# A two-layer hybrid transformer in fp32 on one core: low parts and sums of the FFN moved from GpSimd to VectorE, and the gate product put behind an addition

## The chip, the cores and the metric

The kernel runs on one core of a Trainium2 chip. The number that counts is the device time of one execution in microseconds. A core has five engines with an instruction queue each: TensorE (PE in the rows; its weight loads are PEld), VectorE (DVE), ScalarE (ACT), GpSimd (POOL) and SyncE (SP), which here issues DMAs. Each engine takes its own queue strictly in order and waits on semaphores of the others.

## What is computed

```python
for i in range(2):                       # layer 0: FoX attention, layer 1: MLA attention
    h = rmsnorm(x, norm_mix[i])
    x = x + concat(mixer(h), memory_cross(h)) @ w_out[i]
    h = rmsnorm(x, norm_ffn[i])
    u = h @ w_up[i]                      # (1024, 1024) @ (1024, 5632), fp32
    u = causal_conv3(u) + conv_b         # depthwise, along the sequence
    gate, val = split(u, 2)              # 2816 columns each
    x = x + (silu(gate) * val) @ w_down[i]
```

The change touches the FFN alone, which runs once in each of the two layers.

## The kernel before

**Split products.** A matmul operand in fp32 is split in two: a high part, a copy that ACT rounds, and a low part, the operand minus its high part. A product is then three matmuls, high by high, high by low and low by high. The helper `split(hi, lo, src, he, le)` does it: ACT writes the high part (line 83, CAST), and the engine `le`, DVE ("v") or POOL ("p"), subtracts (line 90). Operands are tiles `f_op` of 128 partitions by 2 x 512 elements.

**Up projection (`FFN.run`, products on PE).** The 2816 columns of gate and of value are cut into 22 chunks of 128. Each chunk is a 2 by 2 block product done with seven block products instead of eight: four sums of weight blocks (S1 to S4, `make_sums`), seven operands (`make_op`), and seven products of 12 matmuls each (`product`). From chunk 1 on their order is `ORDER = (1, 4, 6, 5, 7, 2, 3)`. They accumulate in PSUM banks a, b, c and d. Products 6 and 7 both fill bank b: between them the bank must be read, by the addition u2 = b + p1 (`behind`, k == 6; p1 is a copy of product 1). After product 7 DVE adds u3 and twice into `f_cv` (the value), after product 3 once into `f_cg` (the gate). Then the convolution (`conv`): ACT does one tap (line 881), DVE two (line 883, 128 x 1023 and 128 x 1022), for the gate ACT adds a silu (line 886), and DVE multiplies value and gate (line 93, 128 x 1024, the gate product). The result is stored to `g` in DRAM on the SP queue, behind which the next chunks' weight loads (`f_raw`, line 767) stand.

**Ahead of PE.** `look` makes an operand five products ahead (LOOK = 5), six `f_op` tiles deep. S1 and S2 are on DVE, S3 and S4 and all seven low parts on POOL.

**Down projection.** `down` multiplies g by w_down in three blocks of 4, 4 and 3 chunk pairs; each pair goes through the same seven products, so a layer has 77 products of 12 matmuls. `down_sums` makes the block sums (DVE, 8 for each pair), `dsplit` splits both operands of a product (two low parts, so 154 a layer), two products ahead (`dlook`). After the last pair of each product kind, DVE adds four banks and then four more into x (line 1128, tiles `f_x`), 84 additions a layer, which frees the banks.

**What sets the order.** PE keeps program order. The other engines' queues are ordered by a scheduler from priorities, so a moved instruction can land some rows away from where the code has it; the rows below show where.

Of the kernel before, what the change touches and what calls it, by code (L numbers as in the profile page):

```python
# [12 lines left out]
OP = mybir.AluOpType  # L13
# [18 lines left out]
NCH = DFF // P  # L32
# [42 lines left out]
def hybrid_kernel(ctx: ExitStack, tc: tile.TileContext, A, out):  # L75
    nc = tc.nc
# [4 lines left out]
    def copy(eng, o, i):  # L81
        if eng == "a":
            nc.scalar.copy(o, i)  # L83
        elif eng == "v":
            nc.vector.tensor_copy(o, i)
        else:
            nc.gpsimd.tensor_copy(o, i)

    def sub(eng, o, a, b):
        (nc.vector if eng == "v" else nc.gpsimd).tensor_tensor(o, a, b, op=OP.subtract)  # L90

    def mul(eng, o, a, b):
        (nc.vector if eng == "v" else nc.gpsimd).tensor_tensor(o, a, b, op=OP.mult)  # L93

    def split(hi, lo, src, he="a", le="p"):
        copy(he, hi, src)
        sub(le, lo, src, hi.bitcast(F32))
# [624 lines left out]
    class FFN:  # L722
# [51 lines left out]
        def make_sums(self, c, *names):  # L774
            b = self.blocks(c)
            s = self.sums.setdefault(c, {})
            for n in names:
                s[n] = self.sp.tile([P, 4, P], F32, name=f"f_{n}")
            for n in names:
                if n == "S1":  # L780
                    nc.vector.tensor_tensor(s[n], b["A21"], b["A22"], op=OP.add)  # L781
                elif n == "S2":
                    sub("v", s[n], s["S1"], b["A11"])
                elif n == "S3":
                    sub("p", s[n], b["A11"], b["A21"])
                else:
                    sub("p", s[n], b["A12"], s["S2"])

        def make_op(self, c, k, le="p"):
            n = self.PRODUCTS[k][0]  # L790
            src = self.sums[c][n] if n[0] == "S" else self.blocks(c)[n]
            op = self.op.tile([P, 2, 4, P], F32R, name="f_op")
            split(op[:, 0], op[:, 1], src, "a", le)
            self.ops[c, k] = op

        def taps(self):
# [46 lines left out]
        def behind(self, c, k):  # L843

            acc = self.acc
            tail, head = slice(512, 1024), slice(0, 512)

            def add(o, x, y):
                nc.vector.tensor_tensor(o, x, y, op=OP.add)  # L849

            if k == 1:
                self.p1 = self.pu.tile([P, 512], F32, name="f_p1")
                copy("a", self.p1, acc["a"])
            elif k == 6:
                self.u2 = self.pu.tile([P, 512], F32, name="f_u2", bufs=1)
                add(self.u2, acc["b"], self.p1)
            elif k == 2:
                self.cg = self.cr.tile([P, S], F32, name="f_cg")
                copy("a", self.cg[:, head], acc["a"])
            elif k == 7:  # L860
                self.u3 = self.pu.tile([P, 512], F32, name="f_u3", bufs=1)
                add(self.u3, acc["b"], self.p1)
                self.cv = self.cr.tile([P, S], F32, name="f_cv")
            elif k == 3:
                add(self.cg[:, tail], acc["c"], self.u2)
            self.done.add(k)
            for need, o, x in (({7, 5}, tail, "c"), ({7, 4}, head, "d")):
                if k in need and self.done >= need:
                    add(self.cv[:, o], acc[x], self.u3)
            if self.val is None and self.done >= {4, 5, 7} and (c or k == 3):  # L870
                self.val = self.conv(c, 1, self.cv)
            if k == 3:
                gate = self.conv(c, 0, self.cg)
                mul("v", self.val, gate, self.val)
                self.g[c] = self.val
                self.acc, self.begun, self.done, self.val = {}, set(), set(), None

        def conv(self, c, j, src):
# [29 lines left out]
        def run(self, finish):  # L908
            self.op, self.sp, self.pu, self.cr = (open_pool(n, b, side=self.other) for n, b in
                                                  (("f_op", 6), ("f_S", 1), ("f_pu", 2), ("f_cr", 1)))  # L910
            self.B, self.g, self.pools = {}, {}, []
            self.acc, self.begun, self.done, self.val = {}, set(), set(), None
            self.seq = [(c, k) for c in range(NCH) for k in (self.ORDER if c else self.FIRST)]
            self.plan_down()
            self.hx.release()
# [168 lines left out]
        def dsplit(self, n):  # L1084
            s, k, i = self.dseq[n]
            out = []
            for j in range(2):
                src = self.operand(s, i, self.DOWN[k][j], j)
                hl = (self.op if n < 6 or n % 5 < 3 else self.op2).tile([P, 2, 4, P], F32R, name="f_op").rearrange(
                    "p a b c -> p a (b c)")  # L1090
                split(hl[:, 0], hl[:, 1], src, "a", "v" if j and n % 3 == 0 else "p")
                out.append(hl)
            self.dops[n] = out
            if k == 7:
                self.load_down(s + 1, i, 0)
            if k == 4:
                self.load_down(s + 1, i - (s + 2 == len(self.blocks_of)), 1)
# [567 lines left out]
    for g in range(1, 6):  # L1665
        p = groups[g].pieces()
# [87 lines left out]
```

## Time and profile before

| | |
|---|---|
| runs | 2595.33, 2599.51, 2603.27 us; median 2599.51 |
| the profiled execution | 2597.95 us, its span 2596.2 us, mean clock 0.962 |
| FFN of layer 0 | up projection about 628 to 1090 us of the span, down projection 1090 to 1330 |
| FFN of layer 1 | up projection about 1888 to 2352, down projection 2352 to 2592 |

A time "at 863" is in us from the start of the span. A row of waits says which engine stood still and what ended it. Busy time of PE counts overlapping matmuls once; in a dense run they start 0.23 us apart, though each is shown with 0.39.

### The profile page before, as it was taken

How to read it: one execution, taken by the hardware profiler on the slowest of the kernel's cores; microseconds unless marked ns; L12 is line 12 of the kernel's file. 1: busy time of each engine (PE TensorE's matmuls, PEld its weight loads, DVE VectorE, ACT ScalarE, POOL GpSimd, SP SyncE). 2: the span in 40 equal slices, each digit the busy share in tenths (PEclk: the TensorE clock that was granted, in tenths of full speed). 3: DMA queues.
4: the chain of work that ended last, by engine and by line, in shares of the span. 5: the costliest groups of instructions: out<-in, count | busy, mean ns of one | idle time of the engine just before them, and what ended most of it. 6: DMA issues, size and time to landing. Idle time of an engine off the chain costs nothing.

```text
span 2596.2 us, 32544 instructions
## 1 busy us (share of the span) xinstructions
PE 2391.8 (92%) x11609; PEld 1960.3 (76%) x11609; DVE 1819.7 (70%) x2937; ACT 1203.2 (46%) x2341; POOL 1546.4 (60%) x992
## 2 busy tenths in 40 slices
PE   8999899888999999989998798979989999997999
PEld 7999666667777777767888576757767777776787
DVE  7422788738777677779877868773576776678786
ACT  5544777613444444433454555554254444443343
POOL 1122476723577777678941556665157777776797
PEclk9999899998999999989999899989989999999999
DMA  5210122252222222441330110012312222225221
GB/s 161 59 50 26 34 59 59 61 172 83 66 78 77 90 73 80 180 156 38 106 130 11 34 31 18 19 37 90 132 54 85 73 81 82 82 73 235 81 98 65
DMA packets 163653, 208.91 MB, mean 80 GB/s; under 512 B 11175, under 2 KB 124682, under 8 KB 163490
## 3 DMA queue, kind: packets, MB, share of 16 engines
q1 hardware_dynamic: 162054, 206.63, 25.1%
q8 instruction: 92, 1.51, 0.2%
q14 instruction: 71, 0.58, 0.1%
q10 hardware_dynamic: 1436, 0.18, 0.0%
HBM read 153.34 MB, written 39.98 MB: 74 GB/s over the span
## 4 chain that ended last, share of the span: by engine, by line
PE 47%; DVE 34%; ACT 6%; issue 5%; DMA 4%; POOL 2%; SPq 1%; ACTq 0%; DVEq 0%; POOLq 0%
PE psX L102 19%; PE psS L102 17%; DVE f_v L883 11%; PE psO L102 10%; DVE f_v L93 4%; POOL f_op L90 2%; ACT f_v L881 2%; PE psX L106 2%; ACT f_v L886 2%; DMA rrow<-rec 1%; DVE f_S L781 1%; DVE mA L292 1%; DVE f_S L1071 1%; ACT f_op L83 1%; DVE f_u L849 1%
## 5 line engine op out<-in xcount | busy, mean ns | idle before, releaser
L90 POOL TENSOR_TENSOR f_op<-f_S,f_op 128x512 fp32r<-128x512 f32 x248 | 364.3, 1472 | 287.3 <-ACT f_op L83 287.2
L102 PE MATMUL psS<-f_T,f_op 128*128 128x512 f32 x1584 | 384.6, 394 | 31.1 <-DVE f_u L849 26.1
L90 POOL TENSOR_TENSOR plo<-pf,ph 128x1024 fp32r<-128x1024 f32 (+2 forms) x160 | 313.8, 1972 | 164.6 <-ACT pf L336 99.5
L102 PEld LDWEIGHTS psS<-f_T,f_op 128*128 128x128 f32 x1584 | 293.0, 188 | 106.2 <-issue 38.6
L83 ACT CAST f_op<-f_S 128x512 fp32r<-128x512 f32 x248 | 153.5, 621 | 330.4 <-PE psS L102 143.7
L102 PE MATMUL psX<-f_B,f_op 128*128 128x512 f32 x1260 | 296.0, 389 | 0.0
L102 PEld LDWEIGHTS psX<-f_B,f_op 128*128 128x128 f32 x1260 | 236.5, 188 | 49.2
L90 POOL TENSOR_TENSOR f_op<-f_raw,f_op 128x512 fp32r<-128x512 f32 x146 | 229.1, 1583 | 30.7 <-ACT f_op L83 30.2
L102 PE MATMUL psS<-f_op 128*128 128x512 f32 x960 | 228.1, 396 | 11.2 <-DVE f_x L1128 8.6
L102 PEld LDWEIGHTS psS<-f_op 128*128 128x128 f32 x960 | 182.6, 191 | 53.4 <-DVE f_x L1128 10.3
L883 DVE SCALAR_TENSOR_TENSOR f_v<-f_cg,cw,f_v 128x1023 f32<-128x1023 f32 x88 | 164.0, 1864 | 54.4 <-ACT f_v L881 52.8
L102 PE MATMUL psX<-f_op 128*128 128x512 f32 x666 | 175.7, 406 | 25.9 <-DVE f_op L90 17.8
L90 POOL TENSOR_TENSOR f_op<-f_d,f_op 128x512 fp32r<-128x512 f32 x118 | 175.0, 1502 | 25.4 <-ACT f_op L83 25.1
L102 PEld LDWEIGHTS psX<-f_op 128*128 128x128 f32 x666 | 130.2, 197 | 57.5 <-DVE f_op L90 19.5
L102 PE MATMUL psX<-w_w,hTh 128*128 128x384 f32 (+2 forms) x672 | 167.4, 334 | 2.3 <-ACT hTh L83 2.2
L883 DVE SCALAR_TENSOR_TENSOR f_v<-f_cv,cw,f_v 128x1023 f32<-128x1023 f32 x88 | 151.0, 1716 | 8.7 <-ACT f_v L881 7.3
L335 ACT ACTIVATE ph<-psS 128x1024 fp32r<-128x1024 f32 (+2 forms) x131 | 112.3, 857 | 93.5 <-PE psS L102 84.6
L849 DVE TENSOR_TENSOR f_u<-psS,f_p 128x512 f32<-128x512 f32 x88 | 60.3, 685 | 133.0 <-PE psS L102 133.0
L83 ACT CAST f_op<-f_raw 128x512 fp32r<-128x512 f32 x148 | 90.6, 616 | 116.1 <-issue 42.4
L102 PE MATMUL psX<-KA,QA 66*128 66x128 f32 (+4 forms) x320 | 111.8, 396 | 30.4 <-DVE mA L292 14.1
L90 POOL TENSOR_TENSOR w_w<-w_raw,w_w 128x384 fp32r<-128x384 f32 (+2 forms) x28 | 29.9, 1072 | 176.7 <-ACT w_w L83 176.7
L93 DVE TENSOR_TENSOR f_v<-f_v 128x1024 f32<-128x1024 f32 x44 | 94.8, 2153 | 52.8 <-ACT f_v L886 52.8
(377 smaller groups left out, 5871.1 us busy)
## 6 DMA issues: line engine op xcount, KB each, us to landing
f_raw<-in_ffn_w_up_dram SPq DMA_DIRECT2D x88, 512.0 KB
g<-f_v SPq DMA_DIRECT2D x44, 512.0 KB
f_d<-g SPq DMA_DIRECT2D x36, 512.0 KB
f_d<-in_ffn_w_down_dram SPq DMA_DIRECT2D x36, 512.0 KB
w_raw<-in_fox_w_in_dram SPq DMA_DIRECT2D x48, 192.0 KB
rrow<-rec SPq DMA_DIRECT2D x32, 256.0 KB
wo_raw<-in_w_out_dram SPq DMA_DIRECT2D x32, 256.0 KB
xr<-x SPq DMA_DIRECT2D x16, 512.0 KB
```

Of the source, the lines that this page charges most:

```text
L83: nc.scalar.copy(o, i)
L90: (nc.vector if eng == "v" else nc.gpsimd).tensor_tensor(o, a, b, op=OP.subtract)
L93: (nc.vector if eng == "v" else nc.gpsimd).tensor_tensor(o, a, b, op=OP.mult)
L102: r = nc.tensor.matmul(*a, **k)
L106: r = nc.tensor.transpose(*a, **k)
L292: nc.vector.tensor_reduce(mA[:, q0:q0 + n], px[:, :n * width].rearrange("p (a b) -> p a b", a=n), axis=AX, op=OP.max)
L335: nc.scalar.activation(ph, ps[:, :w], AF.Exp)
L781: nc.vector.tensor_tensor(s[n], b["A21"], b["A22"], op=OP.add)
L849: nc.vector.tensor_tensor(o, x, y, op=OP.add)
L881: nc.scalar.activation(v, src, AF.Identity, bias=cw[:, 3, ch:ch + 1], scale=cw[:, 2, ch:ch + 1])
L883: nc.vector.scalar_tensor_tensor(v[:, k:], src[:, :S - k], cw[:, 2 - k, ch:ch + 1], v[:, k:], op0=OP.mult, op1=OP.add)
L886: nc.scalar.activation(v, v, AF.Silu)
```

## The change

Three low parts of a chunk (products 1, 3 and 4) and the sums S3 and S4 go from POOL to DVE, for all chunks but the first. The gate product of a chunk is kept back and issued right behind the next chunk's addition u2, which then comes first on DVE; for the last chunk it is issued as before. In the down projection the low parts were on DVE for the second operand of every third product (26 of 154 a layer), else on POOL; now they are on POOL only for the first operand where n % 4 is not 0 (57), else on DVE (97).

```diff
                 elif n == "S3":
-                    sub("p", s[n], b["A11"], b["A21"])
+                    sub("v" if c else "p", s[n], b["A11"], b["A21"])
                 else:
-                    sub("p", s[n], b["A12"], s["S2"])
+                    sub("v" if c else "p", s[n], b["A12"], s["S2"])
...
-            split(op[:, 0], op[:, 1], src, "a", le)
+            split(op[:, 0], op[:, 1], src, "a", "v" if k in (1, 3, 4) and c else "p")
...
             elif k == 6:
                 self.u2 = self.pu.tile([P, 512], F32, name="f_u2", bufs=1)
-                add(self.u2, acc["b"], self.p1)
+                u2 = nc.vector.tensor_tensor(self.u2, acc["b"], self.p1, op=OP.add)
+                if self.gated:
+                    with tc.issue_after(u2.ins):
+                        self.gated()
+                    self.gated = None
...
                 gate = self.conv(c, 0, self.cg)
-                mul("v", self.val, gate, self.val)
                 self.g[c] = self.val
+                self.gated = lambda v=self.val: mul("v", v, gate, v)
+                if c == NCH - 1:
+                    self.gated()
...
-                split(hl[:, 0], hl[:, 1], src, "a", "v" if j and n % 3 == 0 else "p")
+                split(hl[:, 0], hl[:, 1], src, "a", "p" if j == 0 and n % 4 else "v")
```

**DVE in a chunk of the up projection, before**, from the two gate taps to the next chunk's sums. Here `f_v<-f_cg` are the taps, `f_v<-f_v` the gate product, `f_u2` and `f_u3` the additions that read bank b.

```order
L883 SCALAR_TENSOR_TENSOR f_v_7141<-f_cg_7121,cw_5733,f_v_7141 128x1023
L883 SCALAR_TENSOR_TENSOR f_v_7141<-f_cg_7121,cw_5733,f_v_7141 128x1022
L93 TENSOR_TENSOR f_v_7098<-f_v_7141,f_v_7098 128x1024
L849 TENSOR_TENSOR f_u2_7198<-psS_7170,f_p1_7163 128x512
L849 TENSOR_TENSOR f_u3_7236<-psS_7170,f_p1_7163 128x512
L849 TENSOR_TENSOR f_cv_7238<-psX_7208,f_u3_7236 128x512
L849 TENSOR_TENSOR f_cv_7238<-psS_7170,f_u3_7236 128x512
L781 TENSOR_TENSOR f_S1_7343<-f_raw_7168 128x512
L90 TENSOR_TENSOR f_S2_7344<-f_S1_7343,f_raw_7269 128x512
```

**The same place after the change** (line numbers are six or seven higher there).

```order
L889 SCALAR_TENSOR_TENSOR f_v_7141<-f_cg_7121,cw_5733,f_v_7141 128x1023
L90 TENSOR_TENSOR f_op_7182<-f_S4_7106,f_op_7182 128x512
L889 SCALAR_TENSOR_TENSOR f_v_7141<-f_cg_7121,cw_5733,f_v_7141 128x1022
L90 TENSOR_TENSOR f_S4_7249<-f_raw_7126,f_S2_7201 128x512
L90 TENSOR_TENSOR f_op_7204<-f_raw_7126,f_op_7204 128x512
L856 TENSOR_TENSOR f_u2_7197<-psS_7169,f_p1_7162 128x512
L93 TENSOR_TENSOR f_v_7098<-f_v_7141,f_v_7098 128x1024
L90 TENSOR_TENSOR f_op_7221<-f_raw_7024,f_op_7221 128x512
L849 TENSOR_TENSOR f_u3_7236<-psS_7169,f_p1_7162 128x512
L849 TENSOR_TENSOR f_cv_7238<-psX_7208,f_u3_7236 128x512
L849 TENSOR_TENSOR f_cv_7238<-psS_7169,f_u3_7236 128x512
L781 TENSOR_TENSOR f_S1_7343<-f_raw_7167 128x512
```

The addition u2 has moved ahead of the gate product; a low part of S4, the sum S4 and a low part of `f_raw` stand between the taps and u2, and another low part behind the gate product.

**POOL over one chunk, before**, from one low part of S1 to the next.

```order
L90 TENSOR_TENSOR f_op_7552<-f_S1_7486,f_op_7552 128x512
L90 TENSOR_TENSOR f_op_7576<-f_S3_7534,f_op_7576 128x512
L90 TENSOR_TENSOR f_S3_7677<-f_raw_7555,f_raw_7454 128x512
L90 TENSOR_TENSOR f_op_7594<-f_raw_7412,f_op_7594 128x512
L90 TENSOR_TENSOR f_op_7612<-f_S4_7535,f_op_7612 128x512
L90 TENSOR_TENSOR f_S4_7678<-f_raw_7555,f_S2_7630 128x512
L90 TENSOR_TENSOR f_op_7633<-f_raw_7555,f_op_7633 128x512
L90 TENSOR_TENSOR f_op_7650<-f_raw_7454,f_op_7650 128x512
L90 TENSOR_TENSOR f_op_7674<-f_S2_7630,f_op_7674 128x512
```

**And after.**

```order
L90 TENSOR_TENSOR f_op_7552<-f_S1_7486,f_op_7552 128x512
L90 TENSOR_TENSOR f_op_7575<-f_S3_7534,f_op_7575 128x512
L90 TENSOR_TENSOR f_op_7593<-f_raw_7412,f_op_7593 128x512
L90 TENSOR_TENSOR f_op_7674<-f_S2_7630,f_op_7674 128x512
```

Nine subtractions a chunk (seven low parts, S3 and S4) have become four low parts.

**DVE at the start of the first down projection, before**, where the operands of the second and third kind of products are made (`f_p1`, `f_u2` and `f_u3` hold block sums of w_down here, `f_S1` to `f_S4` those of g, `f_x` is x).

```order
L90 TENSOR_TENSOR f_op_10035<-f_u3_9991,f_op_10035 128x512
L1071 TENSOR_TENSOR f_S4_10016<-f_d2_9867,f_d6_9879 128x512
L90 TENSOR_TENSOR f_S1_9918<-f_d0_9873,f_S1_9918 128x512
L90 TENSOR_TENSOR f_p1_9919<-f_d1_9874,f_p1_9919 128x512
L90 TENSOR_TENSOR f_d3_9868<-f_d7_9880,f_d3_9868 128x512
L90 TENSOR_TENSOR f_u3_9991<-f_d5_9878,f_u3_9991 128x512
L90 TENSOR_TENSOR f_op_10099<-f_p1_9969,f_op_10099 128x512
L90 TENSOR_TENSOR f_d2_9867<-f_d2_9867 128x512
L90 TENSOR_TENSOR f_S3_9990<-f_S3_9990,f_d0_9865 128x512
L1128 TENSOR_TENSOR f_x0_9884<-f_x0_9884,psS_9932 128x512
```

**The same stretch after**, from the low part of `f_u3` to that of `f_u2`, which the eighth product needs.

```order
L90 TENSOR_TENSOR f_op_10035<-f_u3_9991,f_op_10035 128x512
L90 TENSOR_TENSOR f_p1_9969<-f_d3_9876,f_p1_9969 128x512
L90 TENSOR_TENSOR f_d3_9868<-f_d7_9880,f_d3_9868 128x512
L90 TENSOR_TENSOR f_op_10075<-f_p1_9919,f_op_10075 128x512
L90 TENSOR_TENSOR f_S3_9990<-f_S3_9990,f_d0_9865 128x512
L1134 TENSOR_TENSOR f_x0_9884<-f_x0_9884,psS_9932 128x512
L90 TENSOR_TENSOR f_S1_9918<-f_d0_9873,f_S1_9918 128x512
L90 TENSOR_TENSOR f_d2_9867<-f_d2_9867 128x512
L90 TENSOR_TENSOR f_S2_9968<-f_d2_9875,f_S2_9968 128x512
L1134 TENSOR_TENSOR f_x1_9885<-f_x1_9885,psS_9932 128x512
L90 TENSOR_TENSOR f_u3_9991<-f_d5_9878,f_u3_9991 128x512
L90 TENSOR_TENSOR f_op_10055<-f_u2_10017,f_op_10055 128x512
```

Before, the low part of `f_u2_10017` was POOL's and not in DVE's queue; now it stands eleven rows behind that of `f_u3_9991`, with sums, one other low part and two additions into x between them.

## Rows read from the trace of the kernel before

**Rows 1.** The page of the profile, busy time, share and instructions of each engine.

```profile
PE 2391.8 (92%) x11609; PEld 1960.3 (76%) x11609; DVE 1819.7 (70%) x2937; ACT 1203.2 (46%) x2341; POOL 1546.4 (60%) x992
```

**Rows 2.** Waits, 700 to 1085 and 1960 to 2330: total us, times, longest.

```profile
PE psS L102 <- DVE f_u L849: 12.0, 19, 0.6
...
PE psS L102 <- DVE f_u L849: 11.7, 19, 0.6
```

**Rows 3.** Timeline of one chunk: start, length, engine, line, instruction, idle before.

```profile
860.40 2.88 PE L102 MATMUL psO<-f_T,f_op 128*128 128x512 f32 x12
...
860.77 3.52 POOL L90 TENSOR_TENSOR f_op<-f_raw,f_op 128x512 fp32r<-128x512 f32 x2
...
860.85 2.32 DVE L93 TENSOR_TENSOR f_v<-f_v 128x1024 f32<-128x1024 f32 x1 [1.19 <-ACT f_v L886]
863.09 0.68 DVE L849 TENSOR_TENSOR f_u<-psS,f_p 128x512 f32<-128x512 f32 x1
...
863.91 2.98 PE L102 MATMUL psS<-f_T,f_op 128*128 128x512 f32 x12 [0.63 <-DVE f_u L849]
864.26 1.28 POOL L90 TENSOR_TENSOR f_op<-f_S,f_op 128x512 fp32r<-128x512 f32 x1
...
866.74 2.88 PE L102 MATMUL psX<-f_B,f_op 128*128 128x512 f32 x12
...
869.46 2.88 PE L102 MATMUL psO<-f_B,f_op 128*128 128x512 f32 x12
...
874.57 1.24 ACT L881 ACTIVATE f_v<-f_cg,cw 128x1024 f32<-128x1024 f32 x1 [1.51 <-DVE f_cg L849]
...
879.69 1.06 ACT L886 ACTIVATE f_v<-f_v 128x1024 f32<-128x1024 f32 x1 [1.21 <-DVE f_v L883]
...
883.85 2.98 PE L102 MATMUL psS<-f_T,f_op 128*128 128x512 f32 x12 [0.63 <-DVE f_u L849]
```

**Rows 4.** Instruction groups by shape, DVE, 700 to 1085: busy us, mean ns, idle before.

```profile
L883 DVE SCALAR_TENSOR_TENSOR f_v<-f_cv,cw,f_v 128x1022 f32<-128x1022 f32 x19 | 41.7, 2196 | 0.7
...
L883 DVE SCALAR_TENSOR_TENSOR f_v<-f_cv,cw,f_v 128x1023 f32<-128x1023 f32 x19 | 24.3, 1278 | 1.3 <-ACT f_v L881 1.3
```

**Rows 5.** Windows: length, busy PE, PEld, DVE, ACT, POOL, clock, DMA share, GB/s.

```profile
1090.00:1132.00 42.00, 30.05 (x107) 22.38 (x106) 41.97 (x40) 13.85 (x23) 27.04 (x17) 0.86 0.70 281
...
1198.00:1205.00 7.00, 6.44 (x20) 5.18 (x21) 6.97 (x12) 1.14 (x2) 1.06 (x1) 0.68 0.00 0
1205.00:1330.00 125.00, 124.50 (x552) 102.51 (x551) 101.49 (x132) 55.78 (x97) 112.10 (x74) 1.00 0.24 83
```

**Rows 6.** Waits of PE, 1085 to 1330: total us, times, longest.

```profile
PE psX L102 <- DVE f_op L90: 8.9, 2, 5.1
PE psS L102 <- DVE f_x L1128: 3.8, 2, 3.4
```

**Rows 7.** Waits of the DMA queue SP, 700 to 1085: total us, times, longest.

```profile
SPq L767 <- POOL f_op L90: 208.7, 35, 11.6
```

**Rows 8.** Timeline of the first down projection, its start and second block.

```profile
1111.48 1.77 DVE L90 TENSOR_TENSOR f_S<-f_S,f_raw 128x512 f32<-128x512 f32 x1
...
1113.17 1.76 DVE L90 TENSOR_TENSOR f_d<-f_d,f_d 128x512 f32<-128x512 f32 x1
...
1117.12 0.68 DVE L90 TENSOR_TENSOR f_op<-f_u,f_op 128x512 fp32r<-128x512 f32 x1
...
1117.72 0.68 DVE L1071 TENSOR_TENSOR f_S<-f_d,f_d 128x512 f32<-128x512 f32 x1
...
1117.85 1.22 PE L102 MATMUL psX<-f_op 128*128 128x512 f32 x2 [3.88 <-DVE f_op L90]
...
1131.69 12.59 PE L102 MATMUL psS<-f_op 128*128 128x512 f32 x42 [3.39 <-DVE f_x L1128]
...
1172.30 0.78 DVE L1071 TENSOR_TENSOR f_S<-f_d,f_d 128x512 f32<-128x512 f32 x1 [2.17 <-DMA f_d<-g]
...
1198.56 1.22 PE L102 MATMUL psX<-f_op 128*128 128x512 f32 x2 [5.05 <-DVE f_op L90]
```

More of the change, by code (lines that the diff above doesn't have):

```diff
@@ L784, in make_sums, with make_op @@
                 elif n == "S3":
-                    sub("p", s[n], b["A11"], b["A21"])
+                    sub("v" if c else "p", s[n], b["A11"], b["A21"])
                 else:
-                    sub("p", s[n], b["A12"], s["S2"])
-        def make_op(self, c, k, le="p"):
+                    sub("v" if c else "p", s[n], b["A12"], s["S2"])
+        def make_op(self, c, k):
             n = self.PRODUCTS[k][0]
@@ L911, in run @@
             self.B, self.g, self.pools = {}, {}, []
-            self.acc, self.begun, self.done, self.val = {}, set(), set(), None
+            self.acc, self.begun, self.done, self.val, self.gated = {}, set(), set(), None, None
             self.seq = [(c, k) for c in range(NCH) for k in (self.ORDER if c else self.FIRST)]
```

## The prediction

> **What bounds the kernel now.** The table of busy time comes first: PE is busy 92% of the span, DVE 70%, POOL 60% [rows 1], so what counts is where PE stands still. The waits of the two up projections have PE waiting for one thing only, the addition that reads bank b: 19 times in each window, 12.0 and 11.7 us in all [rows 2]. The timeline of one chunk shows why. The product that fills b is over when the next one starts, at 860.40, and some 0.2 us later the bank could be read; but DVE stands before the gate product, which waits 1.19 us for ACT's silu and then runs from 860.85 for 2.32 us, and the addition stands behind it until 863.09. The product that refills b starts at 863.91, 3.51 us after the one before it, where an undisturbed one takes 2.72 (866.74 to 869.46) [rows 3]. It is 0.11 us longer itself too (863.91 to 866.74 is 2.83). So the chunk takes 19.94 us (863.91 to 883.85) and 7 x 2.72 = 19.04 of it is PE's own.
>
> The second thing to see is that DVE and POOL do not run side by side. The first convolution step (1278 ns) and the second (2196) are the same work [rows 4], and the gate product, as many elements, takes 2.32 us [rows 3]. The long ones are those that meet a POOL instruction: at 860.85 DVE starts while POOL is in the pair of 860.77, and that pair takes 3.52 where one POOL subtraction alone takes 1.28 (864.26) [rows 3]. The addition that reads PSUM (0.68, one operand in SBUF) shows none of it; I take the other four PSUM additions as alike.
>
> In the down projection the windows give 240 us for 77 products of 12 matmuls (3.1 us each, PE needs 2.72), and the loss stands in two places: 1090 to 1132, and 1198 to 1205 at a clock of 0.68; from 1205 to 1330 PE is busy 124.5 of 125 us [rows 5]. The waits there are above all for DVE's low parts (8.9 us) and for the additions into x that free PSUM (3.8) [rows 6]. I take the second layer as alike.
>
> **The change, part by part.** (1) The gate product goes behind the addition that reads b. In the order, three DVE instructions now stand between the convolution's last step and that addition's place: the sum S4 and one low part before it (and another low part and S3 further up), then the addition, then the gate product. To see whether the addition is reached in time, I walk DVE through a chunk with 0 at the start of its first product, so that PE ends products at 2.72, 5.44, 8.16 and 10.88, the third being the one that fills b. DVE enters from the old chunk with u3 at -5.2; u3, two additions, S1, S2 (0.68 each) end at -1.7. Two convolution steps of 1.28 and one collision with POOL (1.09, worked out in (3)) end at 1.95, the addition into cg at 2.6; ACT's tap takes 1.24, to 3.9, while DVE makes S3; then step, low part, step (1.28 + 0.68 + 1.28) end at 7.15, S4 and the low part (0.68 each) at 8.5 [rows 3, 4]. The bank is complete at 8.16 + 0.2. So DVE is there about when the bank is, ends the addition at 9.2, and the product that refills b starts at 10.88: 1.7 us to spare. Meanwhile ACT's silu (1.06, from 7.2) is done at 8.3, so the gate product does not hold DVE either; it ends near 10.4, and a low part follows by 11.1. The next thing that DVE must answer, u3, comes at 13.8.
>
> What waits behind the moved product: the store of g on SP, and behind the store on that queue the weight loads. The gate product ends at 10.4 here, and now, counted from the fourth product's start (860.40, which is 8.16), at 863.17 - 860.40 + 8.16 = 10.9, so the store is not later. The loads wait on POOL's low parts (208.7 us in the window [rows 7]); the last of these moves to DVE and ends at 11.1, where POOL ends it now at 864.29 - 860.40 + 8.16 = 12.1 [rows 3].
>
> Gain: 38 chunks wait [rows 2]. The lower bound is the wait rows themselves, 23.7 us; the upper one the chunk's length, 38 x (19.94 - 19.04) = 34. I take 34, as the walk leaves nothing else for PE to wait for, and PE shows a full clock when it is 99.6% busy (1205 to 1330 [rows 5]).
>
> (2) Three low parts and two sums a chunk move from POOL to DVE. POOL loses 3 x 1.28 + 2 x 1.28 = 6.4 us of work, DVE gains 5 x 0.60 to 0.68 = 3.0 to 3.4. DVE's own work was 5 additions and two sums of 0.68 and five long instructions of 1.28, 11.2 us without collisions; with the five, 14.6. If each of POOL's four remaining subtractions cost it 1.28 more, 19.7: under the present 19.94, over 19.04. In the walk two of the four fall where DVE reads PSUM or is idle. So this part costs nothing while PE's 19.04 covers it; uncovered it costs 0.8 us x 38 = 30, which would take back (1) and no more.
>
> (3) In the down projection 71 low parts a layer move (POOL 128 to 57, DVE 26 to 97, counted from the two rules). Two DVE instructions back to back start 0.60 apart (1117.12, 1117.72); in pairs with POOL's they start 1.69 apart (1111.48, 1113.17) [rows 8]. So a POOL instruction that collides costs DVE 1.09, and the same work on DVE costs it 0.60. Per product, DVE has 88/77 = 1.14 sums and 84/77 = 1.09 additions into x. Counted as if all collide: now (0.34 + 1.14 + 1.09) x 0.60 + 1.66 x 1.09 = 3.35; after (1.26 + 1.14 + 1.09) x 0.60 + 0.74 x 1.09 = 2.90, 223 us for 77 products against the 240 measured. The floor is 77 x 2.72 = 209. So up to 17 to 30 us a layer.
>
> But low parts now stand in one queue with the sums. At the start I walked both orders: the fifth and sixth products get their last low parts when they do now; the eighth gets its second one 11 rows behind the seventh's, 11 x 0.60 + 2 x 1.09 = 8.8 us, so PE's wait there grows from 3.88 (1117.85) to about 6; yet the additions into x that free the next bank, which PE waits for until 1131.69 [rows 8], come some 4 us sooner. Net 4 us. At the second block DVE has 24 instructions from 1172.3 to the low part that PE waits 5.05 us for at 1198.56: 24 x 0.60 + 5 x 1.09 = 20, so it is there at 1192.3, and PE needs it at 1198.56 - 5.05 = 1193.5 [rows 8]. That saves the 5.05 and most of the slow clock's 7 x 0.32 = 2.2; I take 6. Together 10 a layer, bounds 0 (what is saved is lost at the next bank) and 28.
>
> The Trainium skill (SBUF — State Buffer, section on its two separate sides) says that VectorE with two SBUF inputs and GpSimd take the shared ports as an exclusive lock for a whole instruction. The trace agrees in kind; by it a collision would cost 1.28 rather than 1.09, (3) would count 3.49 x 0.60 + 0.74 x 1.28 = 3.04, 234 us, and the gain would shrink to 6.
>
> **Sum.** 2597.95 (the profiled execution, 1.6 below the median shown) - 34 - 2 x 10 = 2544. The span lacks 1.75 of that time, which stays. Chunk 0 of each layer gets a few of the moved instructions too while PE waits for transposed blocks there; 0, within 2 either way.
>
> **Rivals.** (A) The forecast: 2532 to 2560. (B) The up projection gains, the down projection does not: the low parts queue behind the sums. If DVE pays its full 0.68 an instruction [rows 8] instead of 0.60, the count is 3.49 x 0.68 + 0.81 = 3.18, 245 us, 5 over now: 2598 - 34 + 10 = 2574; with no loss 2564. Rows of back-to-back starts speak against it, the eighth product's wait for it. [...] (C) The addition is reached no earlier, because S4 and a low part stand before it and all four POOL subtractions collide: the 1.7 us of room go with two more collisions (2 x 1.09), and with every further one PE waits its 1.09 again: half the up gain left is 2598 - 17 - 10 = 2571, none of it 2588 to 2598. (D) Slower: DVE becomes the bound of the down projection. It decides from 240 + 17 = 257 us a layer on, 3.34 us a product; in the stretches with two sums a product the full count is 4.35 x 0.60 + 0.81 = 3.42, so if those set the pace everywhere, 77 x 3.42 = 263, the time is 2598 - 34 + 46 = 2610. Against it: now the same count is 3.87 there, and PE still runs at 99.6% from 1205 to 1330. (E) The count's full saving in the down projection: 2598 - 34 - 2 x 20 = 2524.
>
> **Chances.** A 0.60, B 0.17, C 0.09 (a third of it within 0.3%), E 0.08, D 0.06. The predicted time is A's, 2544. The range goes from E's to past B's, 2522 to 2578; A's own is 2532 to 2560. 0.3% (7.8 us) is about what a measurement can tell from no change: faster 0.90, same 0.04, slower 0.06.
>
> **What would show it.** Right: no rows of PE waiting for the addition that reads b between 700 and 1085, a chunk of 19.04 us, gate product near 1.2 us; no wait of 5 us at the second block; POOL's share down by a third. Wrong: the addition starting more than 2 us after the third product's end; PE waiting for DVE's low parts in the middle of the down projection; convolution steps still at 2.2 us.

## The result, and the profile after

The changed kernel takes 2536.19 us (median of four runs, 2535.55 to 2536.71); the kernel before takes 2599.2 us beside it (2595.33 to 2603.27). The ratio is 0.9756, 95% interval 0.9742 to 0.9771. The prediction was 2544 us, range 2522 to 2578.

The two profiled executions, cut into stages. A projection's length runs from the start of its first matmul to the start of its last; "the rest" is the span less the four.

| us | up, layer 0 | up, layer 1 | down, layer 0 | down, layer 1 | the rest | span |
|---|---|---|---|---|---|---|
| before | 461.8 | 464.2 | 237.9 | 238.3 | 1194.0 | 2596.2 |
| after | 443.6 | 448.4 | 225.8 | 226.7 | 1189.3 | 2533.8 |
| difference | -18.2 | -15.8 | -12.1 | -11.6 | -4.7 | -62.4 |

The up projections give 34.0 us, the down projections 23.7, and 4.7 lie in code that the change doesn't touch.

The page after, the row that answers to [rows 1]:

```profile
PE 2372.8 (94%) x11609; PEld 1956.4 (77%) x11609; DVE 1905.2 (75%) x3289; ACT 1208.7 (48%) x2341; POOL 975.5 (38%) x640
```

POOL lost 571 us of busy time, 37%, and DVE, which took all that work over, gained only 86. The work is cheaper there, and what was already on DVE got shorter.

**The up projection.** Between 700 and 1065 us, and between 1930 and 2290 in the second layer, there is no row of PE waiting any more; the 19 waits of each window of [rows 2] are gone. The timeline of one chunk after (start, length, engine, line, instruction, idle before), to be laid beside [rows 3]:

```profile
859.27 3.51 DVE L889 SCALAR_TENSOR_TENSOR f_v<-f_cv,cw,f_v 128x1023 f32<-128x1023 f32 x2
...
866.56 1.28 DVE L889 SCALAR_TENSOR_TENSOR f_v<-f_cg,cw,f_v 128x1022 f32<-128x1022 f32 x1
...
867.93 1.06 ACT L892 ACTIVATE f_v<-f_v 128x1024 f32<-128x1024 f32 x1 [0.58 <-DVE f_v L889]
...
869.25 2.88 PE L102 MATMUL psX<-f_T,f_op 128*128 128x512 f32 x12
869.45 0.69 DVE L856 TENSOR_TENSOR f_u<-psS,f_p 128x512 f32<-128x512 f32 x1 [0.40 <-PE psS L102]
...
870.05 1.22 DVE L93 TENSOR_TENSOR f_v<-f_v 128x1024 f32<-128x1024 f32 x1
...
871.97 2.88 PE L102 MATMUL psS<-f_T,f_op 128*128 128x512 f32 x12
...
878.30 3.51 DVE L889 SCALAR_TENSOR_TENSOR f_v<-f_cv,cw,f_v 128x1023 f32<-128x1023 f32 x2
```

The product that fills bank b is over when the next one starts, at 869.25. DVE stands ready 0.40 us for the bank, adds from 869.45 to 870.14, and the refill starts at 871.97, 2.72 us after the product before it. So 1.83 us lie between the end of the addition and the refill, where it was 0.14 before (863.77 to 863.91 [rows 3]). The gate product follows at 870.05 and takes 1.22 us, where it took 2.32. The chunk is 19.03 us long (859.27 to 878.30). The second gate tap is down to 1.28 us; the pair of taps of the value is not (3.51 for the two, so one of them still meets a POOL instruction).

**The down projection.** Waits of PE, 1065 to 1300 us (total, times, longest), against [rows 6]:

```profile
PE psX L102 <- DVE f_op L90: 9.1, 5, 5.8
PE psX L102 <- POOL f_op L90: 1.2, 1, 1.2
PE psS L102 <- DVE f_op L90: 0.2, 1, 0.2
```

Before, in the same view, [rows 6] and two smaller rows:

```profile
PE psX L102 <- POOL f_op L90: 3.7, 2, 2.2
PE psS L102 <- DVE f_op L90: 0.7, 2, 0.5
```

The waits come to 10.5 us, where all four rows of before come to 17.1, and they stand elsewhere. The wait for the additions into x and the one of 5.05 us at the second block [rows 8] are gone; the one at the eighth product has grown. Its rows in the timeline, with DVE's low part that ends it, and that of the seventh product ahead of it:

```profile
1093.91 0.68 DVE L90 TENSOR_TENSOR f_op<-f_u,f_op 128x512 fp32r<-128x512 f32 x1
...
1102.69 0.68 DVE L90 TENSOR_TENSOR f_op<-f_u,f_op 128x512 fp32r<-128x512 f32 x1
```

```profile
1094.64 0.74 PE L102 MATMUL psX<-f_op 128*128 128x512 f32 x2 [1.09 <-DVE f_op L90]
...
1103.42 1.22 PE L102 MATMUL psX<-f_op 128*128 128x512 f32 x2 [5.78 <-DVE f_op L90]
```

Counted product by product in both traces, the down projection of layer 0 is 5.6 us ahead of before when the first twelve products are issued (layer 1: 3.6), and 5.5 (4.9) when thirty are. Then the second block adds 7.2 (7.3), and from there on the lead stays within 0.6 us. Windows after, against [rows 5] (length, busy PE, PEld, DVE, ACT, POOL, clock, DMA share, GB/s):

```profile
1070.00:1112.00 42.00, 31.80 (x119) 23.89 (x118) 40.85 (x53) 15.82 (x26) 16.42 (x9) 0.88 0.72 288
1112.00:1175.00 63.00, 63.00 (x279) 51.99 (x279) 58.13 (x73) 26.31 (x47) 26.57 (x18) 1.00 0.31 100
1175.00:1190.00 15.00, 14.71 (x65) 11.87 (x64) 14.97 (x22) 5.72 (x10) 5.61 (x4) 1.00 0.00 1
```

PE no longer stands still at the second block and the granted clock stays at 1.00 (2.4 GHz) there, where it was 0.68. What is left of the loss is the start: in the first 42 us PE is busy 31.8.

### The profile page after: what moved, and what is told of

Same layout as the page of the kernel before. It is cut to its first block, busy times and chain, and to the rows that moved or that the text cites. A ratio compares the mean times of both kernels' runs of the same rounds, so it can differ in the third digit from the quotient of the medians.

```text
span 2533.8 us, 32572 instructions
## 1 busy us (share of the span) xinstructions
PE 2372.8 (94%) x11609; PEld 1956.4 (77%) x11609; DVE 1905.2 (75%) x3289; ACT 1208.7 (48%) x2341; POOL 975.5 (38%) x640
## 3 DMA queue, kind: packets, MB, share of 16 engines
q1 hardware_dynamic: 162054, 206.63, 25.9%
## 4 chain that ended last, share of the span: by engine, by line
PE 71%; DVE 18%; DMA 4%; issue 3%; ACT 2%; POOL 1%; SPq 1%; DVEq 0%; ACTq 0%; POOLq 0%
PE psX L102 32%; PE psS L102 24%; PE psO L102 14%; DVE f_op L90 2%; DMA rrow<-rec 2%; PE psX L106 2%; DVE mA L292 1%; DVE psX L297 1%; DVE f_x L1134 1%; POOL f_op L90 1%; DVE rs_y L226 1%; DVE KB L517 1%; DVE QB L517 1%; DVE f_T L90 1%; DVE oh L93 1%
## 5 line engine op out<-in xcount | busy, mean ns | idle before, releaser
L90 POOL TENSOR_TENSOR f_op<-f_S,f_op 128x512 fp32r<-128x512 f32 x184 | 270.5, 1472 | 669.2 <-ACT f_op L83 612.0
L102 PE MATMUL psS<-f_op 128*128 128x512 f32 x960 | 222.4, 390 | 0.4 <-DVE f_op L90 0.4
L102 PEld LDWEIGHTS psX<-f_op 128*128 128x128 f32 x666 | 127.3, 193 | 53.9 <-DVE f_op L90 24.4
L83 ACT CAST f_op<-f_d 128x512 fp32r<-128x512 f32 x144 | 84.3, 619 | 102.0 <-PE psS L102 35.6
L849 DVE TENSOR_TENSOR f_u<-psS,f_p 128x512 f32<-128x512 f32 x44 | 30.4, 691 | 126.6 <-PE psS L102 126.6
L102 PEld LDWEIGHTS psX<-w_w,hTh 128*128 128x128 f32 x672 | 121.4, 190 | 3.3 <-ACT hTh L83 3.1
L102 PE MATMUL psS<-QA,KA 67*128 67x512 f32 (+7 forms) x304 | 111.4, 368 | 12.5 <-DMA QA<-mrow 12.4
L889 DVE SCALAR_TENSOR_TENSOR f_v<-f_cg,cw,f_v 128x1023 f32<-128x1023 f32 x88 | 112.7, 1280 | 10.9 <-ACT f_v L887 10.9
L90 POOL TENSOR_TENSOR f_op<-f_d,f_op 128x512 fp32r<-128x512 f32 x52 | 75.5, 1451 | 115.2 <-ACT f_op L83 115.2
```

The costliest lines, as they stand in the source:

```text
L102: r = nc.tensor.matmul(*a, **k)
L889: nc.vector.scalar_tensor_tensor(v[:, k:], src[:, :S - k], cw[:, 2 - k, ch:ch + 1], v[:, k:], op0=OP.mult, op1=OP.add)
```

## The experiments

Two theories of the up projection were to be told apart. The **order theory** is that of the prediction: the addition was late because the gate product stood ahead of it. The **port theory** says it was late because DVE lost time to POOL's subtractions. In the down projection the question was what a low part costs on either engine. All ratios are to the kernel before, timed beside it.

**The gate product's move alone.**

```diff
-                add(self.u2, acc["b"], self.p1)
+                u2 = nc.vector.tensor_tensor(self.u2, acc["b"], self.p1, op=OP.add)
+                if self.gated:
+                    with tc.issue_after(u2.ins):
+                        self.gated()
...
-                mul("v", self.val, gate, self.val)
...
+                self.gated = lambda v=self.val: mul("v", v, gate, v)
...
```

> The gate product of each chunk is issued behind the next chunk's addition that reads bank b, all else as before the change (low parts, sums and the down projection too). Order theory (the addition was late only because the gate product stood ahead of it): the whole gain of the up projections, 34 us, ratio 0.987; up projection of layer 0 about 444 us between its first and last matmul, where before it took 462; no waits of PE for the addition between 700 and 1085 us, though the gate product itself may still take 2.3 us beside POOL. Port theory (the addition was late because DVE lost time to POOL): DVE is still slowed by nine POOL subtractions a chunk, so the delays move to the additions behind the gate product; at most half, 17 us, ratio 0.993 or above.

2565.52 us, ratio 0.9871 (0.9848 to 0.9894). The up projections take 444.8 and 446.7 us, 34.5 less than before, and no wait of PE for the addition is left. POOL still has 278 of 360 us of work between 700 and 1060, and the gate product still collides, as these lines of a chunk show (timeline):

```profile
871.88 1.06 ACT L892 ACTIVATE f_v<-f_v 128x1024 f32<-128x1024 f32 x1 [1.22 <-DVE f_v L889]
872.51 2.88 PE L102 MATMUL psX<-f_T,f_op 128*128 128x512 f32 x12
872.78 0.69 DVE L856 TENSOR_TENSOR f_u<-psS,f_p 128x512 f32<-128x512 f32 x1 [1.00 <-PE psS L102]
...
873.39 1.88 DVE L93 TENSOR_TENSOR f_v<-f_v 128x1024 f32<-128x1024 f32 x1
...
875.23 2.88 PE L102 MATMUL psS<-f_T,f_op 128*128 128x512 f32 x12
```

That is the order theory's number, and the port theory's "at most half" is wrong. The collision is still there (1.88 us instead of 1.22), and nobody waits for it.

**The low parts and sums of the up projection alone.**

```diff
-                    sub("p", s[n], b["A11"], b["A21"])
+                    sub("v" if c else "p", s[n], b["A11"], b["A21"])
...
-            split(op[:, 0], op[:, 1], src, "a", le)
+            split(op[:, 0], op[:, 1], src, "a", "v" if k in (1, 3, 4) and c else "p")
```

(S4 as S3.)

> Three low parts a chunk and the sums S3 and S4 go to DVE, while the gate product stays ahead of the addition; down projection as before. Order theory: the addition still waits behind the gate product, which waits for ACT's silu, so most of the wait stays: gain 0 to 12 us, ratio 0.995 to 1.0. Port theory: with POOL's subtractions gone from beside the convolution the silu comes earlier and the gate product takes 1.2 us; from the chunk after the change (silu over at 868.99, bank complete at 869.25, refill at 871.97) the addition would be over at about 870.9, 1.1 us before the refill: the whole 34 us, ratio 0.987, without the reordering.

2561.27 us, ratio 0.9859 (0.9835 to 0.9883); up projections 442.5 and 449.7 us, 33.8 less. Now it is the order theory's 0 to 12 us that is wrong. A chunk:

```profile
866.09 1.06 ACT L890 ACTIVATE f_v<-f_v 128x1024 f32<-128x1024 f32 x1 [0.59 <-DVE f_v L887]
...
867.18 1.23 DVE L93 TENSOR_TENSOR f_v<-f_v 128x1024 f32<-128x1024 f32 x1
867.39 2.88 PE L102 MATMUL psX<-f_T,f_op 128*128 128x512 f32 x12
...
868.33 0.68 DVE L856 TENSOR_TENSOR f_u<-psS,f_p 128x512 f32<-128x512 f32 x1
...
870.11 2.88 PE L102 MATMUL psS<-f_T,f_op 128*128 128x512 f32 x12
```

The gate product stands ahead of the addition as before the change, but it starts 0.21 us before the product that follows the bank's (867.18 against 867.39; before the change 0.45 us after it, 860.85 against 860.40 [rows 3]) and takes 1.23 us. The addition is over at 869.01, 1.1 us before the refill.

**Both parts of the up projection, the down projection as before.** The full change with the rule of the down projection put back.

> Both parts of the change in the up projection, the down projection as before. Both theories: 34 us less than before, 2564, ratio 0.987; the down projections still 238 us each with the 5 us wait at the second block. If the up projection's change also carries part of what the parts outside the FFN show (4.7 us less after the change than before), it would be 2560.

2562.4 us, ratio 0.9855 (0.9822 to 0.9887); up projections 34.3 us less, down projections 236.1 and 236.3. Together the two parts give what each gives alone.

**The rule of the down projection alone.**

```diff
-                split(hl[:, 0], hl[:, 1], src, "a", "v" if j and n % 3 == 0 else "p")
+                split(hl[:, 0], hl[:, 1], src, "a", "p" if j == 0 and n % 4 else "v")
```

> Only the rule for the low parts of the down projection changes. By the forecast's term 20 us less (2578, ratio 0.992); by the times between first and last matmul of the two down projections in the trace after the change 24 less (2574, ratio 0.991). The wait at the eighth product grows to about 6 us and the 5 us wait at the second block goes, as in the full change. If it were less than 12 us (ratio above 0.9955), the gain of the down projection would hang on what the up projection leaves behind at its end.

2571.07 us, ratio 0.9892 (0.9866 to 0.9918). The down projections take 226.1 and 225.7 us, 24.4 less, where the full change has 23.7; the up projections keep their waits (11.1 us, 18 times, between 700 and 1060). So the gains of up and down add, and the second doesn't hang on the first.

**Only the sums S3 and S4.** To see which part of the port theory counts: low parts back on POOL, gate product ahead of the addition, down projection as before. The line below is against the full change, and the other two parts are put back as well.

```diff
-            split(op[:, 0], op[:, 1], src, "a", "v" if k in (1, 3, 4) and c else "p")
+            split(op[:, 0], op[:, 1], src, "a", "p")
```

> Of the change only the sums S3 and S4 go to DVE; the low parts of the up projection stay on POOL, the gate product stays ahead of the addition, the down projection is as before. Theory that POOL's train of subtractions beside the gate product is what makes it long: without the two sums POOL's next low part begins about 2 us sooner, the gate product takes 1.2 us instead of 2.3, and the addition is in time: 28 to 34 us less, ratio 0.987 to 0.989. Rival, that the silu's lateness counts (the second gate tap still meets a low part of POOL's and takes 2.2 us, and S4 now stands ahead of the gate product): at most 10 us less, ratio 0.996 or above.

2565.93 us, ratio 0.9877 (0.9859 to 0.9895); up projections 33.1 us less. The timeline:

```profile
865.01 2.20 DVE L887 SCALAR_TENSOR_TENSOR f_v<-f_cg,cw,f_v 128x1022 f32<-128x1022 f32 x1
...
868.18 2.88 PE L102 MATMUL psX<-f_T,f_op 128*128 128x512 f32 x12
...
868.84 1.21 DVE L93 TENSOR_TENSOR f_v<-f_v 128x1024 f32<-128x1024 f32 x1
869.12 2.09 POOL L90 TENSOR_TENSOR f_op<-f_raw,f_op 128x512 fp32r<-128x512 f32 x1 [0.75 <-ACT f_op L83]
869.98 0.68 DVE L856 TENSOR_TENSOR f_u<-psS,f_p 128x512 f32<-128x512 f32 x1
...
870.90 2.91 PE L102 MATMUL psS<-f_T,f_op 128*128 128x512 f32 x12
```

The gate tap still collides (2.20 us), so the silu is hardly sooner, and the gate product, with the sum S4 ahead of it now, starts even later against the bank than before (868.84, 0.66 us after the next product's start). Only its length has changed: DVE starts first and now POOL is the one that is long (2.09). That 1.1 us is just enough: the addition ends 0.24 us before the refill starts (870.66 to 870.90), 0.10 more than the 0.14 that lay between them before. The three low parts without the two sums were not run.

**The eighth product's second low part on POOL.** This and the next two runs are the full change with one line of the down projection altered.

```diff
-                split(hl[:, 0], hl[:, 1], src, "a", "p" if j == 0 and n % 4 else "v")
+                split(hl[:, 0], hl[:, 1], src, "a", "p" if (n == 7 if j else n % 4) else "v")
```

> The full change, but the second low part of the eighth product of each down projection is made by POOL (two instructions of 154 a layer go back in both layers together: one each). After the change PE waits 5.8 us for that low part, which DVE makes at 1102.69 though ACT had its high part ready at about 1095.2. On POOL it stands behind the low part of 1094.79 and would be over at about 1097.9. Theory that the order of DVE's queue makes the wait: the row of 5.8 us goes, some 1 to 3 us come back at the tenth and eleventh products, whose low parts DVE makes at 1103.89 and 1108.33: 3 us less a layer, 2530, ratio 0.9735. Rival, that DVE as a whole is behind at the start: the wait only moves two products on, time as after the change, 2536.

2539.83 us, ratio 0.9774 (0.9756 to 0.9793): not faster than the full change (0.9742 to 0.9771). Waits of PE from 1060 to 1290 us:

```profile
PE psX L102 <- DVE f_op L90: 3.2, 4, 1.4
PE psS L102 <- DVE f_x L1134: 3.1, 2, 2.4
PE psX L102 <- POOL f_op L90: 1.6, 2, 1.2
PE psS L102 <- DVE f_op L90: 0.7, 2, 0.6
```

The row of 5.8 us is gone, and the additions into x are late again (3.1 us): the down projection of layer 0 is only 1.3 us shorter than after the full change (224.5 us against 225.8), that of layer 1 1.1. DVE as a whole is behind at the start; one low part less doesn't bring it forward.

**All low parts of the down projection on DVE.**

```diff
-                split(hl[:, 0], hl[:, 1], src, "a", "p" if j == 0 and n % 4 else "v")
+                split(hl[:, 0], hl[:, 1], src, "a", "v")
```

> The full change, and all 154 low parts of a down projection on DVE, none on POOL. By the count of the forecast (0.60 an instruction, 1.09 more for each collision) DVE needs 2.54 us a product and PE 2.72, and at the start nine more low parts (5.4 us) stand against six collisions less (6.5 us): time within 4 us of that after the change, 2532 to 2540. Theory that DVE becomes the bound where a product has two sums (5.09 x 0.60 = 3.05 a product, about 33 products a layer): 11 us more a layer, 2558, with PE waiting for DVE's low parts in the middle of a block.

2527.46 us, ratio 0.9714 (0.9694 to 0.9735): faster than the full change, which I had not expected. Both down projections take 218.9 us in the profiled execution, which took 2517.5 us, 10 less than the three others. The waits of PE that are left, 1060 to 1290 us:

```profile
PE psX L102 <- DVE f_op L90: 5.5, 2, 3.3
PE psS L102 <- DVE f_op L90: 1.6, 1, 1.6
```

All three lie in the first 37 us, and the wait of 5.8 us is not among them, although DVE makes six more low parts for the first eight products. DVE's two low parts that answer to 1093.91 and 1102.69 above are these:

```profile
1090.89 0.69 DVE L90 TENSOR_TENSOR f_op<-f_u,f_op 128x512 fp32r<-128x512 f32 x1
...
1094.50 0.69 DVE L90 TENSOR_TENSOR f_op<-f_u,f_op 128x512 fp32r<-128x512 f32 x1
```

So it was not the number of its own instructions that put DVE behind. From the last addition into `f_cg` (1071.06 after the change, 1069.31 here) to the end of the eighth product's low part DVE makes 38 instructions in 32.3 us after the change, and 39 in 25.9 here. Of the 6.4 us between them, 5.8 are six instructions that a POOL subtraction made longer (five by about 1.09), and 1.15 is one wait of a sum for a low part of POOL's; the extra instruction takes 0.6 back. In layer 1 the two lengths are the same.

**All low parts of the down projection on POOL.** The other end of the same scale.

```diff
-                split(hl[:, 0], hl[:, 1], src, "a", "p" if j == 0 and n % 4 else "v")
+                split(hl[:, 0], hl[:, 1], src, "a", "p")
```

> The full change in the up projection, and all 154 low parts of a down projection on POOL. By the count of the forecast, where every low part on POOL collides: DVE 2.23 x 0.60 + 2 x 1.09 = 3.52 us a product, POOL 2 x 1.69 = 3.38, so 260 to 271 us a layer where it is 226 after the change: 2604 to 2626, and POOL's share of the down projection near 100%. Theory that only about half of them collide and POOL has room at 1.28 a low part: as before the change, 238 a layer, 2560.

2592.49 us, ratio 0.9975 (0.9962 to 0.9988). The down projections take 250.7 and 249.7 us, between the two forecasts (the profiled execution, 2602.19 us, was the slowest of ten). Waits of PE from 1076 to 1328 us, the two largest rows:

```profile
PE psX L102 <- DVE f_x L1134: 16.7, 2, 10.0
PE psX L102 <- POOL f_op L90: 7.6, 4, 2.7
```

Two waits make most of it, and neither is for POOL's low parts. The first, of 10.03 us, in the timeline of DVE, POOL and PE:

```profile
1155.36 17.94 DVE L90 TENSOR_TENSOR f_p<-f_d 128x512 f32<-128x512 f32 x1 [4.46 <-POOL f_op L90]
```

```profile
1155.27 1.31 POOL L90 TENSOR_TENSOR f_op<-f_d,f_op 128x512 fp32r<-128x512 f32 x1
1156.52 1.31 POOL L90 TENSOR_TENSOR f_op<-f_p,f_op 128x512 fp32r<-128x512 f32 x1
...
1170.25 2.50 POOL L90 TENSOR_TENSOR f_op<-f_d,f_op 128x512 fp32r<-128x512 f32 x2
```

```profile
1181.37 1.62 PE L102 MATMUL psX<-f_op 128*128 128x512 f32 x3 [10.03 <-DVE f_x L1134]
```

One DVE sum of 0.68 us is shown with 17.94 us. It starts when POOL is in a train of subtractions, one every 1.25 us, stands through 14 of them, and ends 0.55 us after the train does (1173.30 against 1172.75). The addition into x that PE waits for stands behind it on DVE. A second sum, at 1235.8, takes 19.83 us, and layer 1 shows the same pair (17.95 and 19.63).

**The smallest version, and one without POOL.** Two versions built on that of all low parts on DVE: with only the sums S3 and S4 moved in the up projection (low parts on POOL, gate product ahead of the addition), and with all seven low parts of the up projection on DVE too.

> The smallest version that the runs so far point to: in the up projection only the sums S3 and S4 on DVE (low parts on POOL, gate product ahead of the addition), in the down projection all low parts on DVE. Theory that the change's remaining parts in the up projection give nothing: the same time as the version with the full up projection and all low parts on DVE, 2527, ratio 0.970 to 0.974. Rival, that POOL, which enters the down projection with its low parts of the last chunks, and the gate product's place hold DVE up at the start of the down projection: 3 to 8 us more a layer, ratio 0.975 or above.

> The full change with all 154 low parts of a down projection on DVE, and in the up projection all seven low parts of a chunk on DVE too (chunk 0 apart), so that POOL has next to nothing to do in the FFN. Count of a chunk on DVE: 16 instructions of 512 at 0.60 and five of 1024 at about 1.2, 15.6 us of PE's 19.04, no collisions. Theory that DVE has room: no waits of PE in the up projection, time as with the low parts of the down projection alone, 2523 to 2531, ratio 0.970 to 0.974. Rival, that four more low parts ahead of the additions make DVE late for bank b again: 0.5 us or more a chunk, 20 us, ratio 0.979 or above.

2521.25 us, ratio 0.9703 (0.9684 to 0.9721), and 2522.9 us, ratio 0.9709 (0.9688 to 0.973). Both beat the full change, and neither can be told from the 0.9714 of the version before. Their up projections take 443.9 and 448.1 us, and 443.7 and 447.0; their down projections 218.3 to 218.9. The page of the second of the two:

```profile
PE 2371.9 (94%) x11609; PEld 1962.7 (78%) x11609; DVE 1932.0 (77%) x3571; ACT 1207.3 (48%) x2341; POOL 542.3 (22%) x358
```

634 instructions fewer than before on POOL and 634 more on DVE: DVE's busy time grows by 112 us, POOL's falls by 1004, time blocked by the other engine counted on both sides. DVE has room for all of it.

## Why the prediction was right, and where it was not

**The up projection, 34 us: 34.0 measured, by steps that held.** The walk has DVE at the addition at 8.5, just after the bank; in the trace, on the same scale (869.25 as 8.16), DVE is ready at 7.96, waits for the bank and adds at 8.36 (869.45). It gave 1.7 us to spare (1.83 measured) and the end of the gate product near 10.4 (871.27 is 10.18). The upper of the two bounds, the chunk's length, was the right one. One of the prediction's signs of being wrong did show, and it cost nothing: the value's second tap still takes 2.2 us, and no wait of PE follows from it.

**But the gain was put down to one of two parts that each give all of it.** Step (1) gave the whole 34 us to the gate product's move, and step (2) asked only what the low parts and sums cost, found nothing, and gave them no gain. The runs show that each of the two gives all of it: 34.5 us by the move alone, 33.8 by the low parts and sums, 33.1 by the two sums only, 34.3 by both parts together. What counts is that the addition was only 0.79 us late a chunk (3.51 - 2.72 [rows 3]). The gate product was longer by 1.1 us than it is undisturbed, a number that the prediction had from the same rows, and this alone exceeds the 0.79. I read [rows 3] as "the gate product stands ahead", and did not ask how late the addition would be with the product there at its own length. The rivals had the same gap: none of them was "the reordering isn't needed".

**The down projection, 20 us: 23.7 measured; the places were right, the sizes a little small.** At the start 4 us were forecast a layer (5.6 and 3.6 measured), with the eighth product's wait growing to about 6 (5.8 in layer 0, 4.1 in layer 1) and the additions into x no longer waited for. At the second block 6 were forecast: 7.2 and 7.3, the 5.05 us wait and the whole of the slow clock's 2.2. The run with this rule alone gave 24.4.

**The price of a collision was used as a constant, and it is not one.** The prediction took 1.09 us for each POOL instruction. The trace of before bears that out for single ones, but with all low parts on POOL the count (260 to 271 us) missed the 250 measured, and the largest waits of PE there came not from a sum of small collisions but from two long lock-outs a layer. With all of them on DVE the count (2.54 us a product, under PE's 2.72) came out right. The eighth product's wait belongs here too. The prediction explained it by the eleven rows behind the seventh's low part, 11 x 0.60 + 2 x 1.09 = 8.8, and the trace has 8.78 (1093.91 to 1102.69). That is right as a count, but it leaves out how late DVE is when it comes to these rows. With all low parts on DVE six rows stand there and none collides (3.61 us), and over the whole start DVE makes one instruction more in 6.4 us less. So the wait of 5.78 us came mostly from POOL's subtractions beside DVE, and not from the length of DVE's queue.

**The rivals.** No gain in the down projection (2564 to 2574) and DVE as its bound (2610) are refuted by the down rule alone, and more strongly by all low parts on DVE. The addition reached no earlier is refuted by the chunk's rows. The count's full saving (2524) was not reached by the change; the version with all low parts on DVE reaches 2527, as its count needs no POOL.

**The rest of the miss.** 2544 less 2535.55, the profiled run, is 8.4 us: 3.7 from the down projections, 4.7 from outside the FFN. The latter can't be put down to the change: in the profiles of the experiments the part outside the FFN lies anywhere between 1186 and 1194 us, with the same code. It is 1209 with all low parts on POOL, in an execution 10 us above the median of its runs; the rest of that is not explained.

## What to carry to other kernels

When a queue is late by a small amount each round, write down that amount first and then every saving that would cover it: two edits that each cover 0.8 us do not add, and the smaller edit (here two subtractions moved) is enough. Where VectorE and GpSimd work on SBUF side by side, moving elementwise work to GpSimd can cost VectorE more time than doing it would: here 0.60 us on VectorE replaces 1.28 on GpSimd and a delay of 1.09 or more. And when one wait at a stage's start is removed, look at what was behind it: the eighth product's 5.8 us came back in good part as waits for the additions into x, while taking POOL's low parts away, the shared cause, removed both.

## What the hardware showed that I had not expected

A collision between VectorE and GpSimd can last for many instructions, on either side. In the trace before, no POOL subtraction of 512 elements took over 2.3 us. After the change one in each layer took 5.13 us. The one of layer 0 lasted while DVE started six more of its own, 0.60 us apart; it ended only after DVE had to stop, to wait for just this one, and PE waited 1.2 us for the low part:

```profile
1084.17 5.13 POOL L90 TENSOR_TENSOR f_op<-f_S,f_op 128x512 fp32r<-128x512 f32 x1 [7.90 <-ACT f_op L83]
```

```profile
1087.50 0.68 DVE L90 TENSOR_TENSOR f_d<-f_d,f_d 128x512 f32<-128x512 f32 x1
1089.33 1.77 DVE L90 TENSOR_TENSOR f_S<-f_S,f_raw 128x512 f32<-128x512 f32 x1 [1.15 <-POOL f_op L90]
```

The 17.94 us of the run with all low parts on POOL are the same with the sides exchanged. The Trainium skill (SBUF — State Buffer, the section on its two separate sides) says that the engine that starts first holds the shared ports for its whole instruction and the other blocks. The rows agree that one blocks and does not share, but the wait does not end with the instruction in front: it can go on until the other engine's train has a gap. Not all trains do this: at 869.12 in the run with the sums alone, and in the FFN of the trace before, where no subtraction of 512 elements on POOL took over 2.3 us and none on DVE over 1.9, the waiting engine got in after one instruction. What decides it was not tried, and stays open.
